# The framework's scheduler decides the order of the instructions on another simulation of the core

## The chip, the core and the metric

The kernel runs on one core of a Trainium2 chip. A core has five engines that work side by side: TensorE (PE in the profile) multiplies matrices and transposes, VectorE (DVE) and ScalarE (ACT) work element by element, GpSimd (POOL) does a few memsets here, and SyncE (SP) does nothing but issue DMA transfers. Each engine takes its instructions from its own list, in the order in which the compiled program holds them. An instruction that waits for another engine or for a transfer holds up everything behind it on its engine. The metric is the device time of one execution in microseconds.

## What is computed

The reference is a decoder trunk with two layers on 512 tokens of width 1024. In short:

```python
for l in range(2):
    h = rmsnorm(x)
    p = h @ w_in                                  # one projection, its columns split:
    o = [mla(p0), hgrn2(p1), s5(p2), rwkv7(p3)]   # four token mixers, each 512 wide
    x = x + (sum(sigmoid(gate[m]) * (o[m] @ P[m]) for m in range(4))) @ w_out
    x = x + cross_attn(rmsnorm(x), rmsnorm(mem))  # 4 heads over 256 memory tokens
    x = x + conv_ffn(rmsnorm(x))                  # gate, width-3 conv, silu, up, down
x = rmsnorm(x)
```

HGRN2 and RWKV-7 are recurrences over the tokens that the kernel does in chunks; S5 is a scan; MLA is causal attention. All of it is in float32.

## The kernel before, in words

**Dense products.** Weights come from DRAM in chunks of eight 128x128 blocks (512 KB), always in one fixed order. The class `Ring` holds three buffers of raw chunks and two of converted ones: a chunk is split on ScalarE into `whi` (line 236) and on VectorE into the rest, `wlo` (line 237). Each block is then used in `dense` (lines 329 to 331) by three matmuls, `whi` with the high and the low half of the activations and `wlo` with the high half. So a chunk is 24 matmuls of 512 columns for most products. The results go to two banks of PSUM, tag `mm`.

**The mixer stage.** In each layer the function `mixers` walks through the projection's column blocks in one hand-written order (`PATTERN`). Some of the blocks feed the four mixers, and 32 of them are the merge gates (`gate`, line 557), which no mixer needs. Each mixer is a long chain of small steps that go back and forth between TensorE, ScalarE and VectorE: `rwkv_pair` (four pairs of heads in each layer, first evictions at line 862, last at line 1083), `hgrn_head` (four heads), `s5` (four quarters) and `mla` (four heads, each ending at line 1565). `mla` takes the place in SBUF that the last RWKV pair gives up, so it comes after it. TensorE fills the time between these steps with projection matmuls.

**The rest of the layer.** `merge` multiplies the mixers' results, in the order HGRN2, RWKV-7, MLA, S5, and its matmuls have the activations `oh` and `ol`. Then come the output product, the cross attention and the feed-forward part, which is nearly all dense products.

**Who sets the order.** The kernel writes its instructions down once, with Python loops. The framework records them inside a `TileContext` and on leaving it decides in which order each engine gets them. For that it runs a simulation of the engines: whenever an engine can take an instruction there, it gets the one with the highest priority among those that are ready. Priority is the order of writing, but for blocks that the kernel raises:

```python
def first(self, at=0):
    return self.tc.high_priority(offset=self.tc.cur_priority - at if at >= 0 else -at)
...
with self.first(W0):                # Ring.block: the split of a chunk
...
with self.first(R0):                # R0 = -200
    self.rwkv_pair(l, j, rw, t.get("kr"))
...
with self.first(H0):                # H0 = -500
```

All the semaphores follow from the order. All transfers go through SyncE's one queue, whose order is set in the same way.

## Time and profile before

| what | value |
|---|---|
| time, median of 3 runs | 2758.68 us (2749.64 to 2760.59) |
| the profiled execution | 2759.7 us, its span 2757.8 us |
| matmuls on TensorE | 14112 |
| TensorE busy | 2689.0 us, 98% of the span |
| VectorE, ScalarE busy | 1816.5 us (66%), 1117.5 us (41%) |
| mean granted clock of TensorE | 0.986 of full speed |

The span goes from the first to the last instruction of the profiled execution; the time beside it has what lies around it. Busy is the time in which an engine has at least one instruction in work. Matmuls overlap on TensorE, so a matmul's own duration is longer than the distance between two of them.

### The profile page before, as it was taken

How to read it: one execution, taken by the hardware profiler on the slowest of the kernel's cores; microseconds unless marked ns; L12 is line 12 of the kernel's file. 1: busy time of each engine (PE TensorE's matmuls, PEld its weight loads, DVE VectorE, ACT ScalarE, POOL GpSimd, SP SyncE). 2: the span in 40 equal slices, each digit the busy share in tenths (PEclk: the TensorE clock that was granted, in tenths of full speed). 3: DMA queues.
4: the chain of work that ended last, by engine and by line, in shares of the span. 5: the costliest groups of instructions: out<-in, count | busy, mean ns of one | idle time of the engine just before them, and what ended most of it. 6: DMA issues, size and time to landing. Idle time of an engine off the chain costs nothing.

```text
span 2757.8 us, 37738 instructions
## 1 busy us (share of the span) xinstructions
PE 2689.0 (98%) x14112; PEld 2195.9 (80%) x14112; DVE 1816.5 (66%) x3790; ACT 1117.5 (41%) x1775; POOL 31.0 (1%) x117
## 2 busy tenths in 40 slices
PE   7999999999999999999999999999999999999997
PEld 6878877877788888888887877677878888888886
DVE  6678689775575566546465887788666855664563
ACT  5333353336654443223243333543466534332231
POOL 1000000000000000000000000000000000000000
PEclk9999999999999999999999999999999999999998
DMA  6322233354574233333343221333447632333332
GB/s 198 97 74 68 60 109 93 101 152 149 182 258 125 80 99 98 94 98 100 120 147 94 80 81 56 114 100 115 155 148 229 206 106 69 95 96 99 95 97 77
DMA packets 138664, 318.10 MB, mean 115 GB/s; under 512 B 20464, under 2 KB 41584, under 8 KB 138480
## 3 DMA queue, kind: packets, MB, share of 16 engines
q1 hardware_dynamic: 138480, 315.67, 36.9%
q8 instruction: 112, 1.84, 0.3%
q14 instruction: 72, 0.59, 0.1%
HBM read 265.53 MB, written 45.61 MB: 113 GB/s over the span
## 4 chain that ended last, share of the span: by engine, by line
PE 80%; DVE 12%; DMA 3%; ACT 2%; issue 2%; SPq 1%; DVEq 0%; ACTq 0%
PE mm L329 20%; PE mm L330 20%; PE mm L331 20%; DVE wlo L237 2%; PE rw L1016 2%; PE hg L1381 1%; DVE rdg L924 1%; PE mm L353 1%; PE mm L352 1%; PE mm L351 1%; SPq L319 1%; PE rwy L659 1%; DVE rdg L926 1%; PE rw L659 1%; PE rw L1546 1%
## 5 line engine op out<-in xcount | busy, mean ns | idle before, releaser
L329 PE MATMUL mm<-hh,whi 128*128 128x512 f32 x2144 | 853.9, 399 | 5.4 <-ACT wa L471 2.5
L331 PE MATMUL mm<-hh,wlo 128*128 128x512 f32 x2144 | 852.9, 398 | 1.1 <-DVE wlo L237 1.1
L330 PE MATMUL mm<-hl,whi 128*128 128x512 f32 x2144 | 852.6, 398 | 0.1
L236 ACT ACTIVATE whi<-raw 128x1024 fp32r<-128x1024 f32 (+1 forms) x402 | 417.6, 1040 | 737.6 <-PE mm L330 613.4
L237 DVE TENSOR_TENSOR wlo<-raw,whi 128x1024 fp32r<-128x1024 f32 (+1 forms) x402 | 482.1, 1200 | 309.1 <-ACT whi L236 297.8
L329 PEld LDWEIGHTS mm<-hh,whi 128*128 128x128 f32 x2144 | 406.6, 190 | 89.0 <-ACT wa L471 2.9
L331 PEld LDWEIGHTS mm<-hh,wlo 128*128 128x128 f32 x2144 | 407.0, 190 | 84.9 <-issue 2.2
L330 PEld LDWEIGHTS mm<-hl,whi 128*128 128x128 f32 x2144 | 407.1, 190 | 83.4 <-issue 2.4
L329 PE MATMUL mm<-ah,whi 128*128 128x512 f32 x352 | 136.9, 389 | 0.0
L330 PE MATMUL mm<-al,whi 128*128 128x512 f32 x352 | 136.9, 389 | 0.0
L331 PE MATMUL mm<-ah,wlo 128*128 128x512 f32 x352 | 136.9, 389 | 0.0
L588 DVE TENSOR_TENSOR x<-mm,x 128x512 f32<-128x512 f32 x64 | 44.2, 690 | 123.1 <-PE mm L331 123.0
L329 PE MATMUL mm<-oh,whi 128*128 128x512 f32 x256 | 100.0, 391 | 0.4 <-DVE gin L580 0.4
L330 PE MATMUL mm<-ol,whi 128*128 128x512 f32 x256 | 99.8, 390 | 0.0
L331 PE MATMUL mm<-oh,wlo 128*128 128x512 f32 x256 | 99.7, 389 | 0.0
L711 DVE TENSOR_TENSOR gt<-mm,rstd 128x512 f32<-128x512 f32 x44 | 30.5, 692 | 98.6 <-PE mm L331 94.7
L924 DVE TENSOR_TENSOR rdg<-rdg,rE 128x2 f32<-128x2 f32 (+30 forms) x248 | 84.0, 339 | 3.4
L718 ACT ACTIVATE cv<-cv 128x512 f32<-128x512 f32 x44 | 27.8, 632 | 129.7 <-DVE cv L716 129.7
L331 PEld LDWEIGHTS mm<-ah,wlo 128*128 128x128 f32 x352 | 66.1, 188 | 13.8
L330 PEld LDWEIGHTS mm<-al,whi 128*128 128x128 f32 x352 | 66.1, 188 | 13.7
L329 PEld LDWEIGHTS mm<-ah,whi 128*128 128x128 f32 x352 | 66.1, 188 | 13.6
L721 DVE TENSOR_TENSOR up<-mm,rstd 128x512 f32<-128x512 f32 x44 | 30.4, 691 | 63.9 <-PE mm L331 63.9
(501 smaller groups left out, 4092.1 us busy)
## 6 DMA issues: line engine op xcount, KB each, us to landing
raw<-w SPq DMA_DIRECT2D x384, 512.0 KB, 3.6
g_d<-g SPq DMA_DIRECT2D x64, 256.0 KB, 2.2
gin<-g_d SPq DMA_DIRECT2D x64, 256.0 KB, 3.7
oin<-o_d SPq DMA_DIRECT2D x32, 256.0 KB, 3.7
mt<-memT SPq DMA_DIRECT2D x32, 128.0 KB, 3.3
x<-xT SPq DMA_DIRECT2D x16, 256.0 KB, 5.9
raw<-wm SPq DMA_DIRECT2D x10, 256.0 KB, 2.9
xk_d<-xkt SPq DMA_DIRECT2D x16, 128.0 KB, 2.4
```

What stands on the lines that cost most here:

```text
L236: nc.scalar.activation(out=self.hi, in_=raw, func=AF.Copy)
L237: nc.vector.tensor_tensor(out=self.lo, in0=raw, in1=self.hi.bitcast(F32), op=ALU.subtract)
L329: nc.tensor.matmul(ps[:, :N], hi, xh, start=i == 0, stop=False)
L330: nc.tensor.matmul(ps[:, :N], hi, xl, start=False, stop=False)
L331: nc.tensor.matmul(ps[:, :N], lo, xh, start=False, stop=i == n - 1)
L588: self.nc.vector.tensor_tensor(out=self.x[n], in0=ps, in1=self.x[n], op=ALU.add)
L659: nc.tensor.matmul(out, x, y, start=first and n == 0, stop=last and n == 2)
L711: nc.vector.tensor_tensor(out=gt[:, 2:], in0=ps, in1=rs, op=ALU.mult)
L718: nc.scalar.activation(out=cv, in_=cv, func=AF.Silu)
L721: nc.vector.tensor_tensor(out=up, in0=ps, in1=rs, op=ALU.mult)
L924: V.tensor_tensor(out=tmp[:, :n, :t + 1], in0=M[:, :t + 1, :n].rearrange("p s c -> p c s"), in1=E[:, t, :t + 1].unsqueeze(1).to_broadcast( ...
L1016: PE.matmul(ps[:, cs], x[r0, cs], y[r0, cs], start=True, stop=True)
```

## The change

One argument of the `TileContext` is set. The framework then decides the order on its timeline simulation and no longer on its default model of the engines. The instructions themselves, the tiles, the priorities and the computation stay what they are; which order comes out for each engine, and with it where the waits stand, is no longer given.

```diff
-    with tile.TileContext(nc) as tc:
+    with tile.TileContext(nc, schedule_with_timeline_sim=True) as tc:
         with ExitStack() as ctx:
             Trunk(ctx, tc, A).run(out)
```

## Rows read from the trace of the kernel before

**Rows 1.** The page's first part: span, then busy time, share and instructions by engine.

```profile
span 2757.8 us, 37738 instructions
PE 2689.0 (98%) x14112; PEld 2195.9 (80%) x14112; DVE 1816.5 (66%) x3790; ACT 1117.5 (41%) x1775; POOL 31.0 (1%) x117
```

**Rows 2.** Stretches: length, busy time by engine (instructions), granted clock, DMA share, GB/s.

```profile
0.00:69.00 69.00, 53.96 (x288) 47.63 (x289) 43.12 (x83) 35.68 (x56) 7.55 (x16) 0.90 0.61 197
69.00:759.00 690.00, 671.90 (x3944) 538.65 (x3943) 505.84 (x1305) 299.46 (x525) 6.40 (x23) 0.98 0.35 109
759.00:1449.00 690.00, 688.71 (x3216) 571.70 (x3216) 408.93 (x597) 259.47 (x362) 8.43 (x33) 1.00 0.39 122
1449.00:2111.00 662.00, 642.41 (x3823) 516.72 (x3822) 483.09 (x1254) 292.81 (x515) 6.42 (x23) 0.99 0.35 110
2111.00:2691.00 580.00, 579.23 (x2617) 477.54 (x2616) 349.04 (x512) 216.78 (x302) 2.16 (x22) 1.00 0.38 117
2691.00:2757.80 66.80, 52.83 (x234) 43.70 (x232) 26.48 (x42) 13.28 (x16) 0.00 (x0) 0.89 0.21 71
```

**Rows 3.** TensorE's waits over the whole span: us in total, times, longest.

```profile
PE st L949 <- DVE rdg L930: 6.9, 6, 2.6
...
PE hg L1292 <- ACT s5x L1285: 5.0, 6, 1.6
PE st L866 <- ACT rB L862: 4.9, 2, 2.8
PE mm L329 <- ACT whi L236: 4.5, 3, 2.2
```

**Rows 4.** Timeline of one hand-over in an HGRN2 head: start, length, instruction, idle before.

```profile
151.76 0.41 DVE L1403 TENSOR_TENSOR hkk<-hkk,hdec 128x256 f32<-128x256 f32 x1
...
151.97 0.39 PE L330 MATMUL mm<-hl,whi 128*128 128x512 f32 x1
...
152.32 0.35 PE L1381 MATMUL hg<-hqf,hkk 128*128 128x128 f32 x1
```

**Rows 5.** Timeline of TensorE around one of its longest waits.

```profile
385.94 0.69 PE L949 MATMUL st<-rdg,rab 32*32 32x32 f32 x16 [2.61 <-DVE rdg L930]
...
389.29 0.63 PE L331 MATMUL mm<-hh,wlo 128*128 128x512 f32 x1
```

**Rows 6.** Three short stretches, columns as in rows 2.

```profile
272.00:279.00 7.00, 7.00 (x43) 4.87 (x43) 0.00 (x0) 2.68 (x7) 0.00 (x0) 0.50 0.41 139
387.70:391.10 3.40, 3.40 (x21) 2.75 (x19) 1.50 (x7) 2.53 (x5) 0.00 (x0) 0.51 0.37 95
...
2415.00:2484.00 69.00, 69.00 (x306) 57.11 (x306) 43.59 (x57) 20.98 (x25) 0.61 (x6) 1.00 0.32 96
```

**Rows 7.** Single lines in each layer: ns min/median/max, first and last start us.

```profile
L862 ACT ACTIVATE rB<-st,halves x4: 687/687/688, 75.1 to 406.3; 128x512 f32<-128x512 f32 x4
...
L1083 DVE SCALAR_TENSOR_TENSOR rgg<-rw,vec,rgg x4: 742/751/759, 251.0 to 576.4; 128x512 f32<-128x512 f32 x4
...
L1565 ACT COPY mo<-rwy x4: 568/587/588, 661.6 to 727.0; 128x512 f32<-128x512 f32 x4
...
L329 PE MATMUL mm<-oh,whi x128: 389/389/486, 752.3 to 840.3; 128*128 128x512 f32 x128
...
L1565 ACT COPY mo<-rwy x4: 569/587/588, 2032.8 to 2089.3; 128x512 f32<-128x512 f32 x4
...
L329 PE MATMUL mm<-oh,whi x128: 387/389/497, 2107.2 to 2195.0; 128*128 128x512 f32 x128
```

**Rows 8.** SyncE's waits in front of its transfers: us in total, times, longest.

```profile
SPq L319 <- DVE wlo L237: 1302.5, 311, 17.5
...
SPq L319 <- PE rw L1077: 38.0, 2, 26.9
SPq L319 <- DVE x L736: 36.5, 8, 34.5
```

## The prediction

> **What bounds the kernel now.** The first part of the page comes first: TensorE is busy for 2689.0 of 2757.8 us, VectorE for two thirds, ScalarE for less than half [rows 1]. The kernel is bound by TensorE, and what the order of instructions can move is where TensorE stands still or runs below its speed. So the next view is the table of stretches, cut at the stages [rows 2]. The reader is to subtract TensorE's busy time from each length. The start has 69.00 - 53.96 = 15.0 us of idle time and the end 66.80 - 52.83 = 14.0. The two mixer stages have 690.00 - 671.90 = 18.1 and 662.00 - 642.41 = 19.6, together 37.7. Everything else (merge, output product, cross attention, feed-forward) has 1.3 + 0.8 = 2.1 in 1270 us, at the full clock. There the dense products follow one another and there is hardly a choice of order. So the change is decided in the mixer stages, where small steps are fitted in between projection matmuls.
>
> Two more things cost time there. The granted clock is 0.98 and 0.99, which is 0.02 x 690 + 0.01 x 662 = 20.4 us (the clocks are rounded to hundredths, so give or take 6.8). And the list of waits shows that TensorE's idle time is made of many short pieces: the dearest entry is 6.9 us in six times, and none of these in the mixers is over 2.8 us [rows 3].
>
> **How well the order fits.** The timeline of one hand-over shows what a good order is. VectorE starts the last step of `hkk` at 151.76 and needs 0.41, so it is done at 152.17; TensorE has filled the time with projection matmuls, the last of them started at 151.97, and begins the next step of the head at 152.32 [rows 4]. The order met the true moment to 0.15 us. A bad fit looks like the wait at 385.94: a step of the RWKV pair was placed 2.61 us too early, TensorE stood with projection matmuls ready behind it [rows 5]. And a stop has an echo. Between 387.70 and 391.10 the granted clock is 0.51, which is the lower of the two levels (1.2 against 2.4 GHz), and the same happens from 272 to 279 at 0.50 [rows 6]; the matmul at 389.29 takes 0.63 us [rows 5]. At half the clock, 3.4 us of work cost 1.7 us and 7.0 us cost 3.5. So a bad wait costs its own 2.6 us and 1.7 to 3.5 more, some 4 to 6 us.
>
> **The change part by part.** It removes no instruction and adds none: the 14112 matmuls and their durations stay [rows 1], and so do the transfers. It moves instructions, on all engines and on SyncE's queue, by an amount that no row of before can show. I therefore cost it by its two directions.
>
> A step that is placed too early stops TensorE, at 4 to 6 us for a bad one, as above. The lower bound is that all this goes away: 37.7 + 20.4 = 58.1 us less. Upwards there is no bound but the number of hand-overs. In the code an RWKV pair has about 16 places on its path where TensorE must wait for another engine's result and then be waited for itself; four pairs make 64, and MLA's four heads have four each, so 80 in a layer.
>
> A step that is placed too late costs nothing at once, since TensorE has other work. It delays the mixer. What that may cost is read from the ends: the last MLA head of layer 0 is copied out at 727.0, and the merge, whose third quarter needs it, runs from 752.3 to 840.3 [rows 7]; the third quarter begins at 752.3 + 44.0 = 796.3. So the chain has at most 69.3 us to spare in layer 0, and in layer 1, with 2089.3 and 2107.2 to 2195.0, 2151.1 - 2089.3 = 61.8. Beyond these TensorE runs out of work that it may do.
>
> The order of SyncE's queue moves too. A raw chunk may come late by as much as three raw and two converted chunks cover: 5 x 24 matmuls at 69.00 / 306 = 0.2255 us [rows 6] make 27 us. SyncE's waits of up to 26.9 and 34.5 us [rows 8] show that a single blocked store can be as long as that, so an unlucky order could starve TensorE; each chunk that is missed costs up to 24 x 0.2255 = 5.4 us. I take nothing for it and leave it to the upper end.
>
> Between no loss at all and 80 missed hand-overs in each layer I take the nearest rows. They show what an order costs that misses at a few of many places by up to 2.8 us: 58.1 us for the two stages. A second simulation, whose durations differ from the first's, will in my estimate miss at about as many places more as the first one does now, because the present fit, at 0.15 us, leaves little to improve and every change of a duration in the simulation moves later steps. So the term is one more helping, +58.1 us. The ends and the dense stages stay: 0. The sum is against the profiled execution's own time of 2759.7 us, which lies 1 us above the median of 2758.68: 2759.7 + 58.1 = 2817.8, or 2818 us.
>
> **A measure that would leave more room.** By matmul busy time, 68.8 us of the span are idle [rows 1]. The weight loads (PEld) tell another story: in a feed-forward stretch at full pace they are busy for 57.11 of 69.00 us, 82.8%, over the whole span for 2195.9 of 2757.8, 79.6% [rows 1, 6]. If 82.8% were reachable throughout, the span would be 2195.9 / 0.828 = 2652 us, 106 less. The Trainium skill, Perfetto Trace Analysis, section "Identifying the Most-Contended Engine", holds that matmul busy time is a poor measure of how close TensorE is to its limit and that the weight loads' busy share should be used; by that the floor is near 2654 us and not 2702. I don't follow it for the size, because the mixers' small matmuls have another ratio of load to matmul than the 512-column ones, but it stands among the rivals.
>
> **The rivals.**
>
> Faster by a better fit: the new simulation places the steps nearer to their true moments, or a little later than now. The 37.7 us of waits are there to be removed, and a delay of the steps removes them. Half of the 58.1 us gives 2759.7 - 29.0 = 2731 us; all of it 2702. Against it speaks that the present order already meets the moments closely [rows 4]. A delay d at each of 80 hand-overs is harmless as long as 80 d stays under 62 to 69 us, that is up to 0.8 us or between three and four matmuls.
>
> Much slower, because steps come late: the same delay, but longer. If each hand-over comes 2 us late, nine projection matmuls, a layer's chain is 160 us longer; less the spare 69.3 and 61.8 that is 91 + 98 = 189 us, and less the 58.1 of waits that vanish, 131 us: 2891 us. It decides from d = (58.1 + 131.1) / 160 = 1.2 us, about five matmuls. For it speaks how thin the spare time is against 80 hand-overs; against it, that the four RWKV pairs overlap (the first is finished at 251.0, a pair ends every 108 us until 576.4 [rows 7]), so that not all 64 hand-overs stand in one line.
>
> No difference: the two simulations agree closely enough that waits come and go in equal number, 2760 us. The ratio of work to waits in the dense half of the kernel can't change either way.
>
> Much faster: TensorE is fed so well that the weight loads reach their full share everywhere, 2654 us.
>
> **How the numbers follow.** The forecast, one more helping of waits and low clock, has a chance of 0.36; too late 0.15; no difference 0.19; the better fit 0.26; much faster 0.04. 0.5% of the time is 13.8 us, about what a measurement of this kernel can tell from no change. So slower by over that is 0.51, within it 0.19, faster 0.30. The range is from 2712, which leaves out the much faster case and the last part of the better fit, to 2930, half way out in the late case (d a little over 2.2 us). Given that it gets slower at all, 2774 to 2930 is the likeliest case's own range.
>
> **What would show it.** Right: the same number of matmuls; stretches of the dense half at full pace as before; idle time of TensorE in the mixer stages at about 75 us instead of 37.7, in more pieces of 1 to 3 us at the steps of RWKV, HGRN2 and S5, with clock dips behind them. The late case would show few waits until the gates are used up, the last line 1565 or 1083 later than now by more than 60 us, and then long idle pieces in front of MLA steps or the third quarter of the merge. The better fit would show a mixer stage under 10 us of idle time and a clock of 1.00. The forecast would be wrong if the steps' positions hardly move, or if the ends move: a start or a final normalization that loses or gains more than a few us is in none of the terms.

## The result and the profile after

The changed kernel took 2943.43 us against 2756.64 us of the kernel before in the same series: a ratio of 1.068, 95% interval 1.0655 to 1.0705. (One of its four executions took 7883 us and stays out of the ratio; the median of the other three is 2942.74.) Its profiled execution took 2944.13 us. The page's first part, which answers to [rows 1]:

```profile
span 2942.3 us, 37704 instructions
PE 2733.5 (93%) x14112; PEld 2243.1 (76%) x14112; DVE 1831.4 (62%) x3790; ACT 1123.2 (38%) x1776; POOL 30.9 (1%) x117
```

The span grew by 2942.3 - 2757.8 = 184.5 us. TensorE's idle time grew from 68.8 to 2942.3 - 2733.5 = 208.8 us, by 140.0. Its busy time grew by 2733.5 - 2689.0 = 44.5 us with the same 14112 matmuls. That is the clock: in the trace's clock record TensorE is busy at half the full clock for 63.3 us before and for 156.4 us now, and half of the difference, what the same work takes longer there, is 46.5. So three quarters of the loss are standing still, one quarter is running at the lower clock behind the stops.

Where? The table of stretches, with the columns of [rows 2]; the first three lines have the lengths of lines shown there.

```profile
0.00:69.00 69.00, 54.39 (x289) 42.16 (x290) 44.13 (x84) 37.52 (x58) 7.59 (x16) 0.98 0.59 197
69.00:759.00 690.00, 634.39 (x3764) 526.91 (x3763) 477.39 (x1198) 259.72 (x439) 6.39 (x23) 0.94 0.33 102
759.00:1449.00 690.00, 658.35 (x2914) 535.56 (x2913) 392.49 (x618) 267.82 (x399) 2.15 (x22) 0.98 0.36 111
```

And cut finer, at 69 us:

```profile
69.00:621.00 552.00, 550.47 (x3294) 458.11 (x3293) 391.69 (x1000) 206.56 (x345) 5.35 (x21) 0.99 0.34 105
621.00:690.00 69.00, 44.77 (x333) 39.83 (x331) 47.04 (x109) 19.00 (x36) 0.00 (x0) 0.75 0.16 50
690.00:759.00 69.00, 39.15 (x139) 28.97 (x140) 38.66 (x89) 34.16 (x58) 1.04 (x2) 0.71 0.45 130
759.00:828.00 69.00, 62.53 (x277) 48.72 (x276) 41.07 (x74) 43.65 (x69) 0.00 (x0) 0.99 0.54 168
828.00:897.00 69.00, 52.76 (x205) 38.83 (x205) 40.71 (x85) 31.67 (x63) 0.00 (x0) 0.88 0.47 153
1104.00:1173.00 69.00, 63.89 (x275) 52.61 (x274) 40.29 (x62) 20.50 (x24) 0.60 (x6) 0.93 0.27 84
...
2070.00:2139.00 69.00, 42.96 (x337) 37.66 (x335) 49.99 (x116) 18.40 (x39) 0.00 (x0) 0.73 0.13 35
2139.00:2208.00 69.00, 37.58 (x141) 28.98 (x141) 38.75 (x89) 28.53 (x47) 1.04 (x2) 0.70 0.37 110
```

The dense part runs at full pace elsewhere, as in [rows 6]:

```profile
2691.00:2760.00 69.00, 69.00 (x307) 57.13 (x306) 25.74 (x28) 14.70 (x15) 0.10 (x1) 1.00 0.30 93
```

The reader is to see two halves in each mixer stage. From 69 to 621 us TensorE is as good as never idle: 552.00 - 550.47 = 1.5 us. Then, from 621 to 759, it stands still for 24.2 + 29.9 = 54.1 us and runs at a clock of 0.75 and 0.71. Layer 1 repeats it from 2070 to 2208 with 57.5 us. So TensorE is not short of work while gates and projection last; the mixers are late, and when TensorE's other work is gone it waits for the rest of their chain. The waits of 621 to 900 us name that rest, in the columns of [rows 3]:

```profile
PE hg L1292 <- ACT s5x L1285: 16.9, 2, 15.8
PE st L385 <- DMA krs<-kr: 11.1, 1, 11.1
PE rw L1559 <- ACT pr L1552: 7.7, 4, 4.3
PE mm L329 <- ACT oh L359: 7.2, 3, 6.0
```

The last S5 quarter (15.8 us in one piece), then MLA, which can begin only when the last RWKV pair is through, and the merge. (Why the second line is MLA's, though it names a transfer, stands below under SyncE's queue.) Single lines, which answer to [rows 7] and add the gates:

```profile
L1083 DVE SCALAR_TENSOR_TENSOR rgg<-rw,vec,rgg x4: 749/751/783, 314.2 to 688.5; 128x512 f32<-128x512 f32 x4
L1565 ACT COPY mo<-rwy x4: 574/585/586, 769.2 to 856.7; 128x512 f32<-128x512 f32 x4
L557 ACT COPY g<-mm x32: 564/570/617, 226.2 to 626.8; 128x512 f32<-128x512 f32 x32
L329 PE MATMUL mm<-oh,whi x128: 388/389/793, 755.5 to 908.1; 128*128 128x512 f32 x128
...
L1565 ACT COPY mo<-rwy x4: 572/582/587, 2234.2 to 2317.5; 128x512 f32<-128x512 f32 x4
L329 PE MATMUL mm<-oh,whi x128: 387/389/796, 2213.6 to 2367.0; 128*128 128x512 f32 x128
```

In layer 0 the last RWKV pair ends at 688.5 instead of 576.4, the last MLA head at 856.7 instead of 727.0. The gates, which nobody in the mixers needs, are done by 626.8; before, the last one was copied at 753.2:

```profile
L557 ACT COPY g<-mm x32: 564/568/589, 308.8 to 753.2; 128x512 f32<-128x512 f32 x32
```

One hand-over shows how. The timeline of the same step as in [rows 4], with most of the projection matmuls left out:

```profile
104.08 0.42 DVE L1403 TENSOR_TENSOR hkk<-hkk,hdec 128x256 f32<-128x256 f32 x1
...
104.57 0.39 PE L329 MATMUL mm<-hh,whi 128*128 128x512 f32 x1
...
108.65 0.40 PE L329 MATMUL mm<-hh,whi 128*128 128x512 f32 x1
108.89 1.05 PE L1381 MATMUL hg<-hqf,hkk 128*128 128x128 f32 x8
```

`hkk` is there at 104.50 and the step begins at 108.89: 4.4 us later, with 19 projection matmuls started in between. In [rows 4] it was 0.15 us. To see whether this is the rule I took, for every step of a mixer on TensorE between 69 and 560 us, the time from the end of the last instruction of another engine that wrote one of its operands to the step's start. The median is 1.3 us before and 5.4 us after, 4.1 us or 18 matmuls more. This **lateness** is used below; it is a rough measure, since it goes by names of tiles.

### The profile page after: what moved, and what is told of

The parts are those of the page before. It is cut to its first block, busy times and chain, and to the rows that moved or that the text cites. A ratio compares the mean times of both kernels' runs of the same rounds, so it can differ in the third digit from the quotient of the medians.

```text
span 2942.3 us, 37704 instructions
## 1 busy us (share of the span) xinstructions
PE 2733.5 (93%) x14112; PEld 2243.1 (76%) x14112; DVE 1831.4 (62%) x3790; ACT 1123.2 (38%) x1776; POOL 30.9 (1%) x117
## 4 chain that ended last, share of the span: by engine, by line
PE 83%; DVE 5%; ACT 5%; DMA 4%; issue 1%; SPq 1%; DVEq 0%; ACTq 0%
PE mm L329 21%; PE mm L331 21%; PE mm L330 21%; PE rw L1016 2%; PE hg L1381 1%; PE mm L351 1%; PE mm L352 1%; PE mm L353 1%; SPq L319 1%; PE rwy L659 1%; DVE wlo L237 1%; PE rw L659 1%; PE rw L1035 1%; PE rw L1036 1%; DMA mt<-memT 1%
## 5 line engine op out<-in xcount | busy, mean ns | idle before, releaser
L329 PEld LDWEIGHTS mm<-oh,whi 128*128 128x128 f32 x256 | 49.8, 197 | 38.5 <-ACT oh L359 18.5
```

The lines of the kernel that those rows point to most:

```text
L329: nc.tensor.matmul(ps[:, :N], hi, xh, start=i == 0, stop=False)
```

## The experiments

The framework's timeline simulation, as its source has it, takes instructions from the list of the ready ones ahead of the moment at which they run, for TensorE up to 35. What it has taken keeps its place, also when a step of higher priority becomes ready. The number is a setting of that simulation; no run here tests whether the chip has anything like it. The theory was therefore: a step of a mixer lands behind up to 35 projection matmuls that were taken while it was not yet ready. Rivals were a misjudged order of VectorE, ScalarE or the transfers, the priorities, and simple misses on both sides as forecast.

**Whose order is it? (e1, e2)** The kernel is built twice, and TensorE's order from the first build is imposed on the second, which orders the other engines anew around it. These are the lines of e1; in e2 `True` and `False` are exchanged.

```diff
+    for names in pins.values():
+        for a, b in zip(names, names[1:]):
+            tc.add_manual_dep(by[b], a, dep, reason="pin")
...
+    _, order = build(True)
+    nc, _ = build(False, {e: order[e] for e in ['PE']})
```

> Default model for everything, but TensorE's instructions are held in the order that the timeline simulation gave them; the other engines and SyncE's queue are ordered anew around it. Theory (the loss sits in TensorE's own order, whose steps stand too far behind the projection matmuls): 2900 to 2960 us, MLA's last copy of layer 0 near 857 us as in the changed kernel. Rival (the loss comes from the order on ScalarE, VectorE or SyncE's queue): under 2820 us.

Measured: 2999.43 us, ratio 1.0886 (1.0865 to 1.0907), 39 us above the theory's range and far from the rival's. The last pair ended at 713.7, the last MLA head at 884.4 (not near 857), the gates at 648.4. TensorE's order is enough to make the whole loss without the other engines' orders of the changed kernel, and with those that the default model gives around it the kernel is 56 us slower still.

> The mirror image: the timeline simulation for everything, but TensorE's instructions are held in the order of the kernel before. Theory: 2740 to 2800 us, MLA's last copy of layer 0 near 727 us as before. Rival (ScalarE, VectorE or SyncE's queue): over 2880 us.

Measured: 2849.25 us, ratio 1.0338 (1.0314 to 1.0363); the theory's expectation failed, and the rival's 2880 was not reached either. With TensorE's old order kept, the other engines' new orders cost 2849.25 - 2754.47 = 95 us against the kernel before in the same series: from 69 to 621 us TensorE was idle for 552 - 527.6 = 24.4 us, last pair at 602.8, last MLA head at 775.2, the clock at 0.95. Its stretch:

```profile
69.00:621.00 552.00, 527.59 (x3225) 424.66 (x3224) 412.55 (x1083) 201.11 (x352) 6.82 (x23) 0.95 0.29 88
```

So both mixtures cost time, and TensorE's order is the greater part of the harm but not shown to be all of it. Which displaced instruction is to blame in e2 I did not settle.

**How much is handed over ahead (e3 to e8, e12, e14).** The change stays; only the number for TensorE is set.

```diff
+    import concourse.hw_specs as hw_specs
+    hw_specs.TRN2Spec.ENG_ISSUE_QUEUE_DEPTH[mybir.EngineType.PE] = 8   # 1, 2, 3, 4, 5, 16, 70
     with tile.TileContext(nc, schedule_with_timeline_sim=True) as tc:
```

> Timeline simulation, but in it TensorE's list may run ahead of the engine by 1 instruction and not by 35. Theory (steps come late because some twenty projection matmuls are handed over before each of them): the steps come on time, the gates last longer, MLA's last copy of layer 0 at 715 to 760 us, the time 2720 to 2800 us. Rival (the durations in the timeline simulation are off in general): over 2850 us still.

> As with 1, but TensorE's list may run ahead by 8. Theory: if the delay at a step is 8/35 of the 5.4 us that the changed kernel shows, it is 1.2 us, 80 steps in a layer give 98 us, less the 62 to 69 us to spare, which is 65 us in both layers, less the waits that vanish (58): 2740 to 2800 us. Rival (the window makes no difference): 2940 us.

> Timeline simulation, TensorE's list may run ahead by 4. With 8 the steps started 2.6 us after their operands were there (median in layer 0's mixers; 1.3 before, 5.4 in the changed kernel), which is 1.3 us more than before, and the time was 2819. Theory (lateness by the window, waits if the window is too short, as with 1): steps 1.3 to 2.0 us late, MLA's last copy of layer 0 at 740 to 800 us instead of 805, the time 2760 to 2815 us. Rival (shorter windows only trade late steps for early ones, so that 8 is about the best): over 2820 us, with more waits of TensorE in the first 600 us than with 8.

> The same with 16. Theory: steps between 3.5 and 4.7 us late, the last RWKV result of layer 0 between 659 (with 8) and 689 us (with 35), the time between those of 8 and 35: 2850 to 2920 us. Rival (something else than the lateness makes 35 slow): the time stays within 15 us of 2819 or of 2943.

> The same with 70, twice the simulation's own number. Theory: the steps come later still, 6 us or more, the gates are used up earlier than in the changed kernel, the time 2950 to 3050 us. If the projection matmuls that are ready at one time (two banks of 24) are the true limit, nothing changes: 2930 to 2960 us. Rival (lateness does not set the time): faster than 2930.

> Timeline simulation, TensorE's list may run ahead by 5. With 4 the time was 2756 us, with 8 it was 2819. Theory (the spare time of some 65 us in a layer is used up between 4 and 8): 2750 to 2790 us, MLA's last copy of layer 0 between 734 and 805 us. A version that beats the kernel before would have to be under 2742.

> Timeline simulation with 3 instructions of TensorE handed over ahead. With 4 the time was 2755.67 us and TensorE busy for 546.70 of 552 us in the stretch 69 to 621 at a clock of 1.00, with 1 it was 3701 us with steps that came too early. Theory (the lateness of a step falls with the number, until steps come early and TensorE waits for them): 3 is near the lowest point, 2740 to 2800 us, with more waits in front of steps of RWKV, HGRN2 and S5 than with 4. Rival (early waits set in at once below 4): above 2850 us.

> Timeline simulation with 2 instructions of TensorE handed over ahead. 3 gave 2727.75 us with steps that start 2.2 us (median) after their operands, 1 gave 3701 us. Theory (below the lowest point steps come early and TensorE stands in front of them): 2760 to 3300 us, with waits over 2 us in front of mixer steps (st L949, st L866, hg L1292) that 3 doesn't have. Rival (the lowest point lies at 2): under 2728 us.

What was measured, in order of the number (ratio: to the kernel before in the same series; lateness: median as above; last pair and last head: last start of lines 1083 and 1565 in layer 0; all in us; the kernel before has lateness 1.3, 576.4 and 727.0):

| handed over | run | time | ratio (95%) | lateness | last pair | last head |
|---|---|---|---|---|---|---|
| 1 | e3 | 3701.19 | 1.3434 (1.3409 to 1.346) | 6.5 | 807.6 | 1038.0 |
| 2 | e14 | 2736.19 | 0.9941 (0.9928 to 0.9954) | 1.7 | 562.3 | 712.3 |
| 3 | e12 | 2727.75 | 0.9911 (0.9891 to 0.993) | 2.2 | 582.4 | 721.3 |
| 4 | e5 | 2755.67 | 1.0001 (0.9983 to 1.0019) | 2.2 | 589.4 | 734.2 |
| 5 | e8 | 2774.35 | 1.0072 (1.0053 to 1.0092) | 2.5 | 599.2 | 742.8 |
| 8 | e4 | 2819.44 | 1.0235 (1.0219 to 1.0251) | 2.6 | 659.0 | 805.1 |
| 16 | e6 | 2833.85 | 1.0283 (1.0257 to 1.031) | 3.4 | 678.4 | 816.9 |
| 35 | after | 2943.43 | 1.068 (1.0655 to 1.0705) | 5.4 | 688.5 | 856.7 |
| 70 | e7 | 3077.69 | 1.1164 (1.1127 to 1.1202) | 8.0 | 739.9 | 920.7 |

From 2 upwards lateness never falls, and from 3 upwards time, last pair and last head rise together. One number in the edit, and nothing else, moves the kernel from 3078 us over the changed kernel's 2943 down to below the time before; with 4 the two simulations give the same time. That is the theory's main support.

The sizes support it less. 8 and 70 came out slower than expected, 3, 4 and 16 faster, and with 3 TensorE's idle time from 69 to 621 us is about that with 4 (5.9 for 5.3 us) where more waits were expected. 16 lies 14.4 us above 8, within the 15 us that its expectation had named as the sign of a rival, "something else than the lateness"; 35 and 70, which are slower again, show that the number matters, and leave open how much of the loss goes by the lateness. And the median lateness is no measure of the loss: from 5 to 8 it rises by 0.1 us while the last pair moves by 60, from 16 to 35 by 2.0 us while the last pair moves by 10 and the last head by 40. Why stays open.

With 1 the other side opens. The waits of e3 (in e3 and e4 the kernel's lines are 3 higher than in the others) over the whole span:

```profile
PE st L952 <- DVE rdg L933: 58.8, 6, 18.9
PE hg L1295 <- ACT s5x L1288: 44.7, 12, 8.5
PE mm L332 <- DVE gin L583: 36.9, 17, 4.0
```

TensorE stands in front of steps that are not ready, up to 18.9 us at a time; from 69 to 621 us it is busy for only 425.5 of 552 us, at a clock of 0.75. I had expected 2720 to 2800 us and missed by 900; by its number the run went to the rival (durations that are off in general), which the runs with 2 to 5 answer. Nor are the steps only early: by the table they are also 6.5 us late in the median. The same list for 2, cut to 69 to 621 us, has nothing of that kind:

```profile
PE hgo L329 <- ACT whi L236: 2.3, 1, 2.3
PE st L949 <- DVE rdg L930: 1.3, 2, 0.8
PE hg L1292 <- ACT s5x L1285: 1.1, 1, 1.1
```

so the expectation of e14, with early waits and 2760 us or more, failed too, as did its rival of under 2728. Why the step from 2 to 1 is a cliff stays open.

**A version that beats both kernels.** e12 is the fastest, 0.9% under the kernel before and 7% under the change as made. Its first part and its stretches:

```profile
span 2724.8 us, 37711 instructions
PE 2659.7 (98%) x14112; PEld 2191.6 (80%) x14112; DVE 1809.5 (66%) x3790; ACT 1114.8 (41%) x1775; POOL 30.9 (1%) x117
```

```profile
69.00:621.00 552.00, 546.08 (x3452) 452.21 (x3451) 430.96 (x1141) 221.93 (x382) 6.38 (x23) 1.00 0.33 104
621.00:690.00 69.00, 65.61 (x306) 52.08 (x305) 43.28 (x90) 44.60 (x82) 0.00 (x0) 1.00 0.58 179
```

The first of these stretches in the kernel before:

```profile
69.00:621.00 552.00, 535.84 (x3317) 432.86 (x3315) 426.37 (x1132) 209.84 (x364) 6.40 (x23) 0.97 0.31 95
```

Against [rows 1] its idle time over the whole span is nearly the same, 2724.8 - 2659.7 = 65.1 for 68.8 us. Of the 33 us between the two profiled spans (25 between the medians of the series, 2753.20 and 2727.75) 29.3 are in the busy time, 2659.7 for 2689.0. From 69 to 621 us the short stops of the mixers are fewer, 552 - 546.1 = 5.9 us for 16.2, and the dips of the clock behind them are nearly gone (1.00 for 0.97). By the clock record TensorE is busy at half clock for 20.1 us in place of 63.3, which makes 21.6 of the 29.3 us; the other 7.7 are not placed.

**Not the other engines' numbers, not the priorities (e9, e13, e15).** e9 is e5 with the number 4 for ScalarE and VectorE too; e13 is the changed kernel, and e15 is e12, with the mixers' instructions at the top priority:

```diff
-W0, E0, R0, H0, S0, M0 = (0, 0, -200, -500, 0, 0)
+W0, E0, R0, H0, S0, M0 = (0, 0, 0, 0, 0, 0)
```

> Timeline simulation, run-ahead of 4 for TensorE, ScalarE and VectorE (12 for the latter two so far). Theory (only TensorE has ready work that steps can be queued behind): within 25 us of 2756. Rival (steps are late on ScalarE and VectorE too): 2700 to 2735 us, and faster than the kernel before. If 4 is too short for them, as 1 was for TensorE: over 2800 us.

> The changed kernel with the mixers' instructions at the highest priority of all (R0 and H0 are 0 in place of -200 and -500). Theory (a step can't overtake matmuls that the simulation has already handed to TensorE, whatever its priority): within 30 us of the changed kernel's 2943 us. Rival (the priorities are too low for this simulation): below 2880 us, and the RWKV pairs end more than 40 us earlier than 688.5 us.

> e12 with the mixers' instructions at the highest priority (R0 and H0 are 0). With 35 handed over the same edit gave 2903.58 for 2943 us. Theory (what is handed over sets the lateness, and the dense blocks in front of the mixers' steps have no higher priority often): within 15 us of 2728 us. Rival (with few handed over the priority decides which one is taken next, and steps come earlier): below 2710 us, or above 2760 us if they come too early.

Measured: e9 2767.01 us, ratio 1.005 (1.0031 to 1.0069), as the theory had it. e13 2903.58 us, ratio 1.0551 (1.0528 to 1.0575): 40 us less than the changed kernel, 10 more than the theory allowed and 24 short of the rival. Its lateness is 5.6 us, not less than 5.4, its last pair ends at 673.3 (15 us earlier, where the rival asked for 40), its last head at 836.7. So priority does not bring a step nearer to its operands. The 40 us show at the last MLA head, which starts 20.0 us earlier in layer 0 and 43.6 us earlier in layer 1 (2273.9 for 2317.5). Why MLA gains more than the last pair stays open. e15 2730.97 us, ratio 0.9916 (0.9901 to 0.9932), indistinguishable from e12, as expected.

**Is it the gates alone? (e10, e11)** Both orders, with the projection of the 32 gate blocks left out; the merge takes the sigmoid of the kernel's input `xT` in their place. The gates' copies and stores fall away with them, and MLA's rope tables, which the first gate block set off, are set off by the block `kr`.

```diff
-                out.append(gates.pop(0))
+                gates.pop(0)
...
-        return out + gates
+        return out
...
-        self.dma(g, self.g_d[m, n])
+        self.dma(g, self.A["xT"][n])
```

> The gates' projection is left out (32 blocks, 32 x 24 x 0.2255 = 173 us of matmuls in each layer; the merge takes the sigmoid of the layer's input in their place), default model. TensorE now has too little to do beside the mixers. The mixers' own length sets the end of the stage: MLA's last copy of layer 0 between 690 and 727 us, the time 2560 to 2680 us.

> The same without gates, ordered on the timeline simulation with its own run-ahead of 35. Theory (a step is late only while there are ready matmuls to stand in front of it, and the mixers' projection is still there for the first 400 us): later than the default model's version, but by 30 to 110 us and not by 187. Rival (the chain is slower for another reason, such as ScalarE's and VectorE's order): 160 us or more above it.

Measured: 2641.54 us (ratio 0.9588, 0.9565 to 0.961) with the default order and 2791.61 us (1.0134, 1.0112 to 1.0156) with the timeline order. The difference is 150 us, between what theory (30 to 110) and its opposite expected: a miss. In layer 0 the last pair ends at 557.7 and 616.0, 58 us apart where it was 112 with the gates; the last MLA head at 689.4 and 796.0, 107 us apart for 130, since MLA's four heads now take 796.0 - 694.9 = 101 us instead of 689.4 - 627.9 = 61. The MLA lines of e10 and, below it, of e11:

```profile
L1565 ACT COPY mo<-rwy x4: 579/586/586, 627.9 to 689.4; 128x512 f32<-128x512 f32 x4
```

```profile
L1565 ACT COPY mo<-rwy x4: 576/584/586, 694.9 to 796.0; 128x512 f32<-128x512 f32 x4
```

So the gates are about half of what delays the RWKV pairs. The other half stays without them: steps are still late, by about 4.3 us in the median against 1.5, and the filler left is the projection that the mixers do need; that these blocks are what delays them is argued, not tested. MLA's stretch makes 40 of the 107 us (it was 856.7 - 769.2 = 88 us in the changed kernel, whose gates are used up by then, too); I did not take it apart.

## Why the prediction was wrong

**The bound** was right: TensorE sets the time, its matmuls and the transfers are the same (ScalarE counts one instruction more, a table load: 1776 for 1775), and what moved is its idle time and its clock.

**The step that failed** is the choice between the two directions: "A second simulation, whose durations differ from the first's, will in my estimate miss at about as many places more as the first one does now". This put "one more helping" of early waits, +58.1 us, into the sum, and measured is +184.5 us of another kind. The misses of the new simulation do not fall on both sides. While filler lasts they are nearly all late, by a rule of that simulation (what is taken keeps its place), and the runs with 2 to 70 handed over turn the loss up and down with that one number. The forecast's own signs failed accordingly: the waits of 1 to 3 us at mixer steps did not double, they nearly vanished (1.5 us idle in 552), and in their place came pieces of 15.8 and 11.1 us at the end of layer 0's mixer stage, and the like in layer 1.

**The rival "much slower, because steps come late"** is what happened, down to its signs: few waits until the gates are used up, lines 1083 and 1565 more than 60 us later, then long pieces before MLA and the merge. Its accounting holds roughly. In layer 0 the chain is 856.7 - 727.0 = 129.7 us longer; less the spare 69.3 that gives 60.4, and the merge in fact ends 67.8 us later (908.1 for 840.3 of [rows 7]). The last matmul of layer 0's feed-forward part starts 82.1 us late (1466.5 for 1384.4), so layer 1 begins that much late. Its last head is 2317.5 - 2089.3 = 228.2 us later, so its own chain is 146.1 us longer, less 61.8 makes 84.3; its merge ends 172.0 us later (2367.0 for 2195.0), 89.9 more than the 82.1. So the formula gives 60.4 + 84.3 = 144.7 us, and the two layers lost 67.8 + 89.9 = 157.7 up to the ends of their merges. The other 26.8 of the 184.5 us come after the merges. The rival's formula, a delay at each of 80 hand-overs, does not hold as written: 64 x 4.1 us would be 262 us at the last pair, and measured are 112. That fits what the prediction said against this rival, that the pairs overlap. Its turning point was near the mark all the same. It put it at 1.2 us of extra delay; 0.9 us (3 or 4 handed over) gave 0.9% faster and no difference, 1.2 us (5) gave 0.7% slower, 1.3 us (8) gave 2.35% slower. With a formula that is off by more than two, that is in part luck. The chance of 0.15 was too low because I took the good fit of [rows 4] as evidence about the new order. It was one hand-over, at 0.15 us, and not even typical of the old order, whose median lateness is 1.3 us.

**The price of a stop** was read too low in one place. The dip of the clock at 272 us does not end at 279, where the prediction's stretch of [rows 6] is cut, but goes on to 288.8, so its 17.1 us of work cost 8.5 us and not 3.5:

```profile
279.00:289.00 10.00, 10.00 (x50) 7.15 (x49) 1.98 (x2) 3.18 (x5) 0.10 (x1) 0.51 0.28 79
```

**The better fit** exists too, but with 2 or 3 handed over, at 2736 and 2728 us; the prediction had 2731 for half of it.

**The ends and the dense stages** were put at 0. The ends are right: the start's idle time is 69.00 - 54.39 = 14.6 us (15.0 before). The rest is not quite: after the merges 14.3 us are lost in layer 0 and 12.5 in layer 1. Most of it is at the feed-forward part's beginning, 1104 to 1173 us, which has 5.1 us of idle time and a clock of 0.93, together about 10 us, and so again in layer 1 (2553 to 2622 us). With 8 handed over this place lies earlier, from 1035 to 1070 us, and has 1.9 us of idle time and a clock of 0.95.

**SyncE's queue**, left out of the sum, shows little cost of its own, though no run isolates it. The list of waits over the whole span has one converted weight chunk in each layer that came late:

```profile
PE hgo L329 <- ACT whi L236: 11.5, 2, 6.5
```

That is 6.5 us at most for one, near the 5.4 us that the prediction had for a missed chunk. The 11.1 us that the list puts down to `krs` belong to the late chain. The step behind them needs `sq`, which VectorE had ready at 698.75 + 0.69 = 699.44 us:

```profile
698.75 0.69 DVE L373 TENSOR_TENSOR sq<-sq 128x512 f32<-128x512 f32 x1 [1.37 <-ACT sq L370]
699.55 0.77 PE L385 MATMUL st<-ones,sq 128*128 128x1 f32 x3 [11.08 <-DMA krs<-kr]
```

`sq` is made from `cq`, which SyncE began to load at 692.54 us, 4 us after the last RWKV pair (688.5); the transfers of `krs` landed only at 700.4 us or later.

**The weight loads' share** settles nothing here. By it the best version stands at 2191.6 / 2724.8 = 80.4%, the kernel before at 79.6%, the changed one at 76.2%. The loads' time hardly differs, 2191.6 to 2243.1 us, so the share falls as the span grows and says little more than the span. No run came near the 82.8% of a feed-forward stretch, and the 2652 us worked out from it (the prediction also writes 2654) were not reached. The Trainium skill, Perfetto Trace Analysis, section "Identifying the Most-Contended Engine", names the loads' busy share as one of two measures of how close TensorE is to its limit; here it puts the three kernels in the right order.

## What to carry to other kernels

When one engine that takes its list in order has both a long chain of small steps and filler work, look at how late the steps start after their operands, not only at where the engine waits: here filler committed ahead showed an engine that was hardly ever idle for 550 us, and the bill came when the filler was used up. Work out roughly how much delay the chain can bear (spare time over the number of hand-overs; it overstates the delay where chains overlap), and test it by varying how far ahead work is committed. The top priority gave back 40 of 187 us here, and both mixtures of one engine's order with the other engines' orders from another schedule cost time. Filler is a stock: in the fastest kernel here the last gate was copied at 723.0 us and the last mixer head at 721.3, in the changed one at 626.8 and 856.7.

## What the runs showed of the hardware

A fourth of the loss, 44.5 us, and most of the gain of e12, 29.3 of 33 us, are in TensorE's busy time with the same matmuls, so a list of waits does not show them. The prediction had given the clock 20.4 of its 58.1 us. The timeline after the feed-forward part's stops (3.7 us, then the 1.4 of the first line) shows how it comes about:

```profile
1116.49 0.80 PE L329 MATMUL mm<-hh,whi 128*128 128x512 f32 x1 [1.40 <-DVE gt L711]
1117.08 0.63 PE L330 MATMUL mm<-hl,whi 128*128 128x512 f32 x1
1117.51 0.63 PE L331 MATMUL mm<-hh,wlo 128*128 128x512 f32 x1
```

and the table of stretches for the same place:

```profile
1115.00:1120.00 5.00, 3.60 (x9) 2.84 (x9) 3.41 (x6) 2.50 (x3) 0.10 (x1) 0.50 0.00 1
```

Matmuls of 512 columns follow one another every 0.43 us there, at the lower of the two clocks (1.2 GHz, the granted clock of 0.50 in the line above), where at full clock (2.4 GHz) 306 fit into 69 us, 0.2255 us each. The Trainium skill, TensorE: Matmul & The Clock Gate, section "Wait — 56ns, not 53.3ns?", gives 0.4267 and 0.2157 us for these two; the trace agrees with the first, and at full clock is 4.5% slower in this kernel. No run here shows why.
